# A two-layer hybrid decoder trunk: whole weight blocks in one split, gates ahead of their output block, four query blocks' values in one group

## The chip, the core and the metric

One core of a Trainium2 chip runs the whole program. Five engines work side by side, each through its own instruction stream in order: TensorE (PE: matrix products and transposes), VectorE (DVE), ScalarE (ACT), GpSimd (POOL) and SyncE (SP), which here issues the DMAs. They meet through semaphores that the framework sets from the program's reads and writes. The metric is the device time of one execution in microseconds (us). For the kernel before it is 1511.56 us, the median of three runs from 1508.65 to 1513.46.

## The reference

The input is x (512 positions x 1024 channels, f32) and a memory of 256 tokens. Two layers follow each other, and everything within one reads the same x:

```python
for l in range(2):
    h = x @ w_in[l]            # one wide projection; its columns feed all branches
    (rw_p, rw_g, q_lat, kv_lat, k_pe, mla_g, conv_u, conv_g, xq, xg, merge) = split(h)
    y_rwkv = rwkv7(rw_p, ...) * silu(rw_g)         # 8 heads x 64, recurrent state
    y_mla  = causal_attention(q_lat, kv_lat, k_pe) * silu(mla_g)   # 8 heads
    y_conv = swish(ln(conv31(glu(conv_u)))) * silu(conv_g)         # 31 taps
    y_mem  = cross_attention(xq, mem) * silu(xg)   # 4 heads, 256 memory tokens
    proj   = einsum('bsnc,ncd->bsnd', [y_rwkv, y_mla, y_conv, y_mem], w_o[l])
    gates  = sigmoid(merge.reshape(512, 4, 1024) + b_gate[l])
    merged = sum(gates * proj, axis=2)
    x = layer_norm(alpha * x + merged @ w_out[l])
```

A branch's output is 512 wide. For each of the four branches the merge thus needs eight gate projections (128 channels each, over all 1024 channels of x) and eight output projections (128 channels each, over the branch's 512). The causal attention runs over four blocks of 128 queries; block i reads i + 1 blocks of 128 keys.

## The kernel before, in words

**Precision.** Every large product is f32 made of two parts: a value is split into hi (a cast to the matrix engine's reduced f32) and lo (the rest), and `mm3` issues three matmuls: lo x hi, hi x hi, hi x lo, in some order. So each weight block must be split before it can be used: one cast on ACT for hi, one subtraction on DVE for lo (`split`).

**Layout.** Channels lie on the partitions and the 512 positions on the free axis. A projection of 128 channels (`project`) is eight steps over x's channels, three matmuls of 512 columns each, into one PSUM bank. Weights come from HBM as blocks of 128 x 1024 (128 x 640 for a pair of attention heads, 128 x 672 for the latents, which are called w0 to w3 at the start). `weights` issues the DMA into one of two raw buffers (tag "wr") and splits the block part by part: before, a 1024-column block is two parts of 512, each with its own tile in a ring of six (tags "wh", "wl", `WH = 6`), its own cast and its own subtraction. A raw buffer is free for the next DMA when all parts are split; a slot of the ring is free (`free()`) when the matmuls that use the part have been issued.

**Order.** The order of instructions on each engine is decided when the program is written out. A planner (`Plan`) keeps an estimated clock for each engine, holds a list of tasks (Python generators), and lets the next one emit its instructions by its clocks, due times and the conditions that a task yields. `stream` runs the items (projections, gates, merge blocks) one after another; tasks such as the attention's blocks, the splits, the convolution's taps (`cacc`) or the recurrence are put between their steps. `prefetch`, `get` and `weights` run some blocks ahead of the item that uses them. What an engine got in this order it executes in this order on the chip: an instruction that has to wait holds up all that stand behind it on its engine. A change of a rule or of an instruction's size can therefore move instructions anywhere in the program.

**Attention.** A pair of heads hh (four pairs in each layer) projects pq and pk, casts them to xqh/xql and xkh/xkl, and sends them by DMA into per-head tiles qT and kT. The rotary parts, qrh/qrl, come by DMA too. For each block of 128 queries i and head h, `mla_block` makes scores ms{hh}{h}{i}, a softmax mP{hh}{h}{i}, four or fewer transposes mt{hh}{h}{i} on PE, and a copy of the transposed weights to mPT on ACT. When query blocks 0 and 1 of both heads are done, 6 matmuls of 128 columns go to the output bank mo{hh}, and when blocks 2 and 3 are done, 14 more. The copies go to four buffers of 128 x 512, shared by both heads. The cross-attention's tiles begin with x: xs (scores), xP, xt, xPTh/xPTl, xo; its query projection is ps_xq with outputs xqh/xql too, and its memory projections are ps_mk (keys) and pmv (values).

**Merge.** `merge_items` takes for a branch n (0 recurrence, 1 attention, 2 convolution, 3 memory) and each d2 from 0 to 3 two gate projections ps_m{n}{d} (tanh on ACT into tm{n}{d}, two buffers under the tag "tg") and one block of w_o for two output projections po{n}{d}. DVE then forms (tm + 1) * po and adds it to merged{d}. Before, for d2 = 0 and n other than 3, both gates come first (gate, gate, po, po); in all other places the order is gate, po, gate, po. PSUM has two banks under the name pp for projections (ps_..., po, pmv), two under pa, and four or two under pg for the attention and others.

**End of a layer.** `end_items` opens with `start`, an item of the stream that waits until the recurrence has come far enough ("rwkv"), then issues the DMAs of the residual input and of the norm's parameters at once.

In the profile nearly all ACT, DVE and POOL instructions carry the line of one helper (L235), the matmuls L286, the transposes L291 and the DMAs L298, so work is named by its tiles. Layer 1's names end in _1, layer 0's in _0.

## Time and profile before

| | |
|---|---|
| time, median of three runs | 1511.56 us (1508.65 to 1513.46) |
| the profiled execution's own time | 1509.62 us |
| its span, first to last instruction | 1507.8 us |
| mean granted TensorE clock | 0.998 |
| PE busy | 1475.7 us, 98% of the span |
| PE weight load busy (beside PE) | 1237.5 us, 82% |
| DVE busy | 1072.6 us, 71% |
| ACT busy | 688.1 us, 46% |
| POOL busy | 134.3 us, 9% |
| DMA | 153.54 MB, mean 102 GB/s |

PE is busy nearly the whole time, so only two things move the end: how long PE's own work takes, and the 32 us in which PE stands still. Of these some 6 us lie ahead of its first matmul and some 10 us behind its last. What the other engines do matters only where PE waits for it. The list of what PE waits for names for each wait the tile that PE was about to write and, behind the arrow, the engine and tile that released it. A wait of an engine for PE costs nothing. In a timeline row the columns are the start, the duration, the engine, the operation with its output, inputs and shape, the number of instructions in the row, and in brackets the engine's idle time just before with what ended it. SPq rows are DMA issues.

### The profile page before, as it was taken

To read this page: it belongs to the slowest core of one execution; us is meant where nothing else is said; L and a number is where in the kernel's file an instruction comes from. 1 tells how busy PE (TensorE), PEld (TensorE's weight loads), DVE (VectorE), ACT (ScalarE), POOL (GpSimd) and SP (SyncE) were. 2 spreads that over 40 slices of the span, in tenths; PEclk is the share of its full clock that TensorE was granted. 3 is DMA by queue.
4 is the path that set the end of the run, shared out by engine and by line. 5 is a ranking of instruction groups with operands and counts; after the bars stand their busy time and mean duration, and the time that the engine had idled before them with its cause. 6 is when DMAs were issued, how large, how long until landed. Compare 5 with 4: busy or idle time off the path is not lost.

```text
span 1507.8 us, 29728 instructions
## 1 busy us (share of the span) xinstructions
PE 1475.7 (98%) x11896; PEld 1237.5 (82%) x11896; DVE 1072.6 (71%) x2231; ACT 688.1 (46%) x1507; POOL 134.3 (9%) x329
## 2 busy tenths in 40 slices
PE   8998999999999999999999999999999999999997
PEld 8887788888888888888999877888887888888886
DVE  5787998765758576555554889997866586757847
ACT  5544654345254454444255546533444354444432
POOL 0000000020403021000010000000030202020002
PEclk9999999999999999999999999999999999999999
DMA  6334333223232322433343242432232323234331
GB/s 212 119 115 98 105 100 98 96 77 95 62 86 81 95 88 81 140 98 120 121 144 114 83 126 68 121 109 93 82 98 69 94 74 94 65 104 142 126 119 63
DMA packets 89018, 153.54 MB, mean 102 GB/s; under 512 B 41008, under 2 KB 47152, under 8 KB 88880
## 3 DMA queue, kind: packets, MB, share of 16 engines
q1 hardware_dynamic: 88880, 151.65, 33.9%
q8 instruction: 93, 1.52, 0.4%
q14 instruction: 45, 0.37, 0.1%
HBM read 134.32 MB, written 5.77 MB: 93 GB/s over the span
## 4 chain that ended last, share of the span: by engine, by line
PE 91%; DVE 4%; DMA 2%; ACT 2%; issue 1%; SPq 0%; POOL 0%; ACTq 0%; DVEq 0%; POOLq 0%
PE ps_m L286 23%; PE po L286 12%; PE ps_xg L286 3%; PE ps_cg L286 3%; PE ps_rg L286 3%; PE ps_k L286 3%; PE ps_mg L286 3%; PE ps_v L286 3%; PE ps_r L286 3%; PE ps_val L286 3%; PE ms L286 2%; PE pz L286 2%; PE ps_glu L286 2%; PE ps_xq L286 2%; PE pl L286 2%; PE x L286 2%
## 5 line engine op out<-in xcount | busy, mean ns | idle before, releaser
L235 DVE SCALAR_TENSOR_TENSOR cacc<-hpad,prm,cacc 128x512 f32<-128x512 f32 x240 | 178.8, 747 | 3.3
L235 ACT ACTIVATE tm<-ps_m,prm 128x512 f32<-128x512 f32 x64 | 44.1, 689 | 141.2 <-PE ps_m L286 141.1
L235 DVE SCALAR_TENSOR_TENSOR mt<-tm,po 128x512 f32<-128x512 f32 x48 | 32.9, 686 | 71.2 <-PE po L286 69.0
L235 POOL TENSOR_TENSOR ZT<-ZT,tmpW 64x14 f32<-64x14 f32 (+6 forms) x112 | 42.7, 382 | 8.8
L235 ACT ACTIVATE mP<-ms,nmm 128x512 f32<-128x512 f32 (+3 forms) x64 | 33.7, 528 | 18.2 <-DVE nmm L235 17.4
L235 POOL TENSOR_TENSOR tmpW<-ZT,W 64x14 f32<-64x14 f32 (+6 forms) x112 | 39.3, 351 | 8.1
L235 POOL TENSOR_SCALAR ZT<-W 64x256 f32<-64x256 f32 x8 | 4.2, 524 | 383.8 <-DMA W<-scr 383.8
L235 ACT COPY mPT<-mt 128x512 f32<-128x512 f32 (+3 forms) x64 | 26.7, 428 | 22.2 <-PE mt L291 17.0
L235 DVE TENSOR_TENSOR merged<-merged,mt 128x512 f32<-128x512 f32 x48 | 33.5, 697 | 1.7
L235 POOL MEMSET D<- 128x8 f32 x8 | 1.1, 135 | 346.6 <-PE ms L286 327.1
L235 DVE TENSOR_REDUCE nmm<-ms 128x1 f32<-128x512 f32 (+3 forms) x64 | 29.9, 483 | 0.5
L291 PE MATMUL mt<-cst,mP 128*128 128x128 f32 x160 | 27.1, 277 | 2.4 <-DVE mP L235 2.3
L235 DVE TENSOR_SCALAR mP<-mP,smm 128x512 f32<-128x512 f32 (+3 forms) x64 | 24.8, 387 | 2.3
L235 DVE SCALAR_TENSOR_TENSOR merged<-tm,po 128x512 f32<-128x512 f32 x16 | 11.0, 687 | 20.8 <-PE po L286 19.1
L235 POOL TENSOR_SCALAR lrs<-lmv 128x1 f32<-128x1 f32 x8 | 2.5, 315 | 258.4 <-DVE lmv L235 256.7
L291 PEld LDWEIGHTS mt<-cst,mP 128*128 128x128 f32 x160 | 18.6, 141 | 8.0 <-ACT mo L235 2.2
L235 ACT ACTIVATE z<-z,lnb,lrs 128x256 f32<-128x256 f32 (+1 forms) x16 | 9.6, 648 | 31.1 <-DVE lnb L235 31.1
L235 ACT ACTIVATE yb<-yb,mr,gr 128x64 f32<-128x64 f32 x64 | 22.1, 428 | 2.7 <-DVE mr L235 2.7
L286 PE MATMUL ms<-kTl,qT 96*128 96x512 f32 (+3 forms) x64 | 22.3, 348 | 0.0
L286 PE MATMUL mo<-mPT,v 128*64 128x128 f32 x320 | 21.4, 278 | 0.5 <-ACT mPT L235 0.5
L235 POOL TENSOR_SCALAR gr<-gm 128x8 f32<-128x8 f32 x8 | 1.6, 198 | 215.5 <-DVE gm L235 215.5
L286 PEld LDWEIGHTS mo<-mPT,v 128*64 128x64 f32 x320 | 17.3, 136 | 4.0 <-issue 2.9
(3536 smaller groups left out, 5344.5 us busy)
## 6 DMA issues: line engine op xcount, KB each, us to landing
w<-in_w_ch_dram SPq DMA_DIRECT2D x146, 512.0 KB, 3.7
w<-in_w_o_dram SPq DMA_DIRECT2D x32, 512.0 KB, 3.7
w<-in_w_out_dram SPq DMA_DIRECT2D x16, 512.0 KB, 3.8
w<-in_w_lat_dram SPq DMA_DIRECT2D x16, 336.0 KB, 3.2
w<-in_w_mk_dram SPq DMA_DIRECT2D x8, 512.0 KB, 3.5
w<-in_w_mv_dram SPq DMA_DIRECT2D x8, 512.0 KB, 3.4
w<-in_w_qk_dram SPq DMA_DIRECT2D x8, 320.0 KB, 3.1
x<-in_xT_dram SPq DMA_DIRECT2D x8, 256.0 KB, 5.7
```

Source lines behind the costliest of these rows:

```text
L235: return self.plan.keep(f(*a, **k))
L286: plan.keep(nc.tensor.matmul(o, lhsT, rhs, start=start, stop=stop))
L291: plan.keep(nc.tensor.transpose(o, i, ident))
```

## The change

It has five parts, in one diff.

1. **Splits over the whole block.** A block is one cast and one subtraction over all its columns (up to 1024), into one of three slots of 128 x 1024 (`WH = 3`, the same space). The slot is free when all its parts are used; `free` now takes the tile and counts. The last four blocks of all (w_out, `last`) keep their parts.
2. **Both gates ahead of their output block** in every place of `merge_items`: gate, gate, po, po, and the weight blocks are asked for in that order.
3. **The attention's values of four query blocks in one group**: 20 matmuls to mo{hh} once all eight blocks of a pair are done, not 6 and then 14. The copies go to tiles of 384 columns (blocks 0 and 1, two buffers for each head) and 896 columns (blocks 2 and 3, one buffer for each head); a pair's copies to the latter wait until the pair before it has issued its group.
4. **`turn`** lets a branch's splits start when 8, not 6, outputs of the branch ahead of it are merged.
5. **The end's opening** is a task of its own, and its DMAs are spaced by 3000 and 2000 units of the planner's clock; the stream no longer waits for "rwkv" there.

The order of the emitted instructions shifts in many places. Three of them follow; a name's digits are as in the words above.

ACT, first pair of layer 0, where the copies of the transposed weights mPT of the pair's last blocks (003 and 013) stand beside those of the next pair (1..). Before:

```order
L235 COPY mPT003_0_1684<-mt003_0_1673 128x512
L235 CAST xPTh01_0_1707<-xt01_0_1672 128x512
L235 COPY mPT100_0_1710<-mt100_0_1696 128x128
L235 ACTIVATE mP110_0_1703,smm110_0_1705<-ms110_0_1686,nmm110_0_1704 128x128
L235 COPY mPT013_0_1730<-mt013_0_1712 128x512
L235 ACTIVATE mP101_0_1733,smm101_0_1735<-ms101_0_1723,nmm101_0_1734 128x256
L235 COPY xy0_0_1773<-xo0_0_1732 128x512
L235 ACTIVATE mP111_0_1776,smm111_0_1778<-ms111_0_1737,nmm111_0_1777 128x256
L235 COPY mo0_0_1784<-mo0_0_1365 128x512
```

And now:

```order
L235 COPY mPT002_0_1495<-mt003_0_1542 128x512
L235 CAST xPTh00_0_1572<-xt00_0_1556 128x512
L235 COPY mPT012_0_1529<-mt013_0_1564 128x512
L235 COPY mPT100_0_1577<-mt100_0_1571 128x128
L235 ACTIVATE mP110_0_1615,smm110_0_1617<-ms110_0_1579,nmm110_0_1616 128x128
L235 ACTIVATE mP101_0_1619,smm101_0_1621<-ms101_0_1580,nmm101_0_1620 128x256
L235 COPY mo0_0_1640<-mo0_0_1263 128x512
```

The copy of block 013 now goes into a tile that it shares with block 012 and not into a buffer that an earlier block must give back first; mPT100, which took a buffer ahead of it, comes behind it.

SP, the first two pairs of layer 1, where the DMAs of their queries and keys stand with those of weight block w148. Before:

```order
L298 DMA qTl01_1_10165<-xql_1_10190 64x512
L298 DMA w148_10218<-in_w_ch_dram 128x1024
L298 DMA qT10_1_10224<-qrh0_1_10025 32x512
L298 DMA qTl10_1_10225<-qrl0_1_10026 32x512
L298 DMA qT11_1_10226<-qrh0_1_10025 32x512
L298 DMA qTl11_1_10227<-qrl0_1_10026 32x512
L298 DMA kTh0_1_9283<-xkh_1_10220 64x512
L298 DMA kTh1_1_9285<-xkh_1_10220 64x512
```

And now:

```order
L298 DMA w148_9602<-in_w_ch_dram 128x1024
L298 DMA qT10_1_9611<-qrh0_1_9422 32x512
L298 DMA qTl10_1_9612<-qrl0_1_9423 32x512
L298 DMA qT11_1_9613<-qrh0_1_9422 32x512
L298 DMA qTl11_1_9614<-qrl0_1_9423 32x512
L298 DMA qT00_1_9557<-xqh_1_9585 64x512
L298 DMA qT01_1_9559<-xqh_1_9585 64x512
L298 DMA qTl00_1_9558<-xql_1_9586 64x512
L298 DMA qTl01_1_9560<-xql_1_9586 64x512
L298 DMA kTh0_1_8739<-xkh_1_9607 64x512
```

The weight block and the next pair's rotary queries moved ahead of the first pair's qT, so that nothing but the first pair's own transfers stands between xqh and kT.

ACT, layer 1, the merge of the memory branch (n = 3) at d = 2 and 3, with tanh rows tm32 and tm33 and the convolution's tglu3. Before:

```order
L235 ACTIVATE tm32_1_11770<-ps_m32_1_11727,prm1_8273 128x512
L235 CAST w165h0_11775<-w165_11773 128x512
L235 CAST w165h1_11795<-w165_11773 128x512
L235 CAST w166h0_11802<-w166_11800 128x512
L235 CAST w166h1_11820<-w166_11800 128x512
L235 ACTIVATE tm33_1_11838<-ps_m33_1_11799,prm1_8273 128x512
```

And now:

```order
L235 ACTIVATE tm31_1_10904<-ps_m31_1_10830,prm1_7809 128x512
L235 CAST w161h_10909<-w161_10907 128x1024
L235 CAST w162h_10948<-w162_10946 128x1024
L235 ACTIVATE tglu3_1_10980<-ps_glu3_1_10945 128x512
L235 CAST w163h_11008<-w163_11006 128x1024
L235 CAST lhw_1_10990<-raww_1_10999 128x512
L235 CAST lha_1_10991<-rawa_1_11000 128x512
L235 ACTIVATE tm32_1_11043<-ps_m32_1_11005,prm1_7809 128x512
L235 CAST w164h_11049<-w164_11047 128x1024
L235 ACTIVATE tm33_1_11082<-ps_m33_1_11046,prm1_7809 128x512
```

tglu3, which stood ahead of the whole merge, now stands between tm31 and tm32. It keeps its "tg" buffer until the projection of the convolution's values, which follows this merge on PE, so that tm32 and tm33 take turns in the other one.

The diff's core:

```diff
-WH = 6
+WH = 3
@@ weights
-            for i, (w, c) in enumerate(zip(ws, parts)):
-                if last:
-                    h, lo = (u(f"{name}{n}{i}", 512, F32R) for n in "hl")
-                else:
-                    while wlive["hl"] == WH:
-                        yield lambda: wlive["hl"] < WH
-                    wlive["hl"] += 1
-                    h = wp.tile([128, 512], F32R, tag="wh", name=f"{name}h{i}")[:, 0:c]
-                    lo = wp.tile([128, 512], F32R, tag="wl", name=f"{name}l{i}")[:, 0:c]
-                yield from split(h, lo, raw[:, e:e + c])
...
+            else:
+                while len(wlive["hl"]) == WH:
+                    yield lambda: len(wlive["hl"]) < WH
+                h, lo = (wp.tile([128, 1024], F32R, tag=f"w{n}", name=f"{name}{n}") for n in "hl")
+                wlive["hl"][h.tensor.name] = len(parts)
+                yield from split(h[:, 0:cols], lo[:, 0:cols], raw)
+                for w, c in zip(ws, parts):
+                    w.extend((h[:, e:e + c], lo[:, e:e + c]))
+                    e += c
@@ free
-    def free(n=1):
-        wlive["hl"] -= n
+    def free(h):
+        n = h.tensor.name
+        wlive["hl"][n] -= 1
+        if wlive["hl"][n] == 0:
+            del wlive["hl"][n]
@@ mla_block
-            if i > 1:
-                PT = m("mPT" + q, 512, "mPT", 4)
-            else:
-                if h not in two:
-                    two[h] = m("mPT" + q, 512, "mPT", 4)
-                PT = two[h][:, 128 * i:]
-            PT = two[h, i] = PT[:, 0:n]
-            S.copy(PT, ps)
+            if (h, i // 2) not in two:
+                if L["pairs"] < hh - 1 + i // 2:
+                    yield lambda: L["pairs"] >= hh - 1 + i // 2
+                two[h, i // 2] = m("mPT" + q, 896, f"mPW{h}", 1) if i > 1 else m("mPT" + q, 384, f"mPT{h}", 2)
+            e = (0, 128, 0, 384)[i]
+            S.copy(two[h, i // 2][:, e:e + n], ps)
...
-            if len(done) < 4:
+            if len(done) < 8:
                 return
             yield "small"
-            for b in (i - i % 2, i - i % 2 + 1):
+            for b in range(4):
@@ turn
-            return n == 3 or added[{1: 3, 2: 1, 0: 2}[n]] >= 6
+            return n == 3 or added[{1: 3, 2: 1, 0: 2}[n]] >= 8
@@ merge_items
-                        while len(ts) <= (1 if d2 == 0 and n != 3 else b):
+                        while len(ts) < 2:
                             ts.append((yield from gate(get, 2 * d2 + len(ts))))
...
-                blocks = [(A["w_ch"][l, CH_M + 8 * n + 2 * d2], (512, 512)), (A["w_o"][l, n, d2], (512, 512)), (A["w_ch"][l, CH_M + 8 * n + 2 * d2 + 1], (512, 512))]
-                if d2 == 0 and n != 3:
-                    blocks = [blocks[0], blocks[2], blocks[1]]
+                blocks = [(A["w_ch"][l, CH_M + 8 * n + 2 * d2], (512, 512)), (A["w_ch"][l, CH_M + 8 * n + 2 * d2 + 1], (512, 512)), (A["w_o"][l, n, d2], (512, 512))]
@@ end_items
             def start(get):
+                plan.spawn(opening())
+                yield
+
+            def opening():
                 yield lambda: "rwkv" in L
...
                     for i in range(zn):
                         DMA(E["z"][tb][i], TOK[l][:, tb, zw * i:zw * i + zw])
+                    plan.t += 3000.0
+                    yield
```

More of the change, by code (lines that the diff above doesn't have):

```diff
@@ L428, in split @@
         V.tensor_tensor(out=dst_l, in0=src, in1=dst_h.bitcast(F32), op=ALU.subtract)
-    wlive = {"raw": 0, "hl": 0}
+    wlive = {"raw": 0, "hl": {}}
     def weights(name, src, parts, last=False):
@@ L442, in run @@
             e = 0
-            for i, (w, c) in enumerate(zip(ws, parts)):
-                if last:
-                    h, lo = (u(f"{name}{n}{i}", 512, F32R) for n in "hl")
-                else:
-                    while wlive["hl"] == WH:
-                        yield lambda: wlive["hl"] < WH
-                    wlive["hl"] += 1
-                    h = wp.tile([128, 512], F32R, tag="wh", name=f"{name}h{i}")[:, 0:c]
-                    lo = wp.tile([128, 512], F32R, tag="wl", name=f"{name}l{i}")[:, 0:c]
-                yield from split(h, lo, raw[:, e:e + c])
-                e += c
-                w.extend((h, lo))
+            if last:
+                for i, (w, c) in enumerate(zip(ws, parts)):
+                    h, lo = (u(f"{name}{n}{i}", c, F32R) for n in "hl")
+                    yield from split(h, lo, raw[:, e:e + c])
+                    e += c
+                    w.extend((h, lo))
+                    yield
[7 more added lines that the diff above has]
+                    w.extend((h[:, e:e + c], lo[:, e:e + c]))
+                    e += c
                 yield
@@ L486, in project @@
             if k % 4 == 3:
-                free()
+                free(h)
             if k < 7:
@@ L502, in wide @@
                     yield
-            free()
+            free(h)
     def narrow(get, cols, blocks, name, lhs, after):
@@ L517, in narrow @@
                 if b == blocks - 1 and k % 2:
-                    free()
+                    free(h)
                 if k in (1, 3, 5):
@@ L1278, in run @@
                             yield
-                    free()
+                    free(h)
                 if nb == 0:
@@ L1374, in token_blocks @@
                     if tb == 3:
-                        free()
+                        free(w[i][0])
                 yield
@@ L1440, in run @@
                         yield
-                    free()
+                    free(w[0])
                     plan.spawn(heads(T, ps, n, s, there))
@@ L1464, in pair @@
             yield
-            left = [2]
+            two, done = {}, []
             for i in range(4):
-                if i % 2 == 0:
-                    two, done = {}, []
                 for h in range(2):
@@ L1472, in pair, with mla_block @@
                     L["jobs"] += 1
-                    plan.spawn(mla_block(hh, h, i, (qT[h], kT[h]), mo, two, done, left))
+                    plan.spawn(mla_block(hh, h, i, (qT[h], kT[h]), mo, two, done))
                     yield
             L["turn"] += 1
-        def mla_block(hh, h, i, T, mo, two, done, left):
+        def mla_block(hh, h, i, T, mo, two, done):
             n = 128 * i + 128
@@ L1512, in mla_block @@
             done.append(q)
-            if len(done) < 4:
+            if len(done) < 8:
                 return
             yield "small"
-            for b in (i - i % 2, i - i % 2 + 1):
+            for b in range(4):
                 for kb in range(b + 1):
                     for half in range(2):
+                        e = (0, 128, 0, 384)[b] + 128 * kb
                         MM(mo[HALF[half], 128 * b:128 * b + 128], vtok[kb][:, 128 * hh + 64 * half:128 * hh + 64 * half + 64],
-                           two[half, b][:, 128 * kb:128 * kb + 128], start=kb == 0, stop=kb == b)
-            left[0] -= 1
-            if left[0] == 0:
-                L["pairs"] += 1
-                yield
-                yo = u(f"mo{hh}" + t_)
-                S.copy(yo, mo)
-                pg.free()
-                ymla.append(yo)
-                if len(ymla) == 4:
-                    close_phase()
-                    L["mla"] = True
+                           two[half, b // 2][:, e:e + 128], start=kb == 0, stop=kb == b)
+            L["pairs"] += 1
+            yield
+            yo = u(f"mo{hh}" + t_)
+            S.copy(yo, mo)
+            pg.free()
+            ymla.append(yo)
+            if len(ymla) == 4:
+                close_phase()
+                L["mla"] = True
         merged = [None] * 8
@@ L1598, in run @@
                                 yield
-                        free()
+                        free(wh)
                         if merged[d] is None:
@@ L1641, in start @@
             def start(get):
+                plan.spawn(opening())
+                yield
+            def opening():
                 yield lambda: "rwkv" in L
@@ L1649, in start @@
                         DMA(E["z"][tb][i], TOK[l][:, tb, zw * i:zw * i + zw])
+                    plan.t += 3000.0
+                    yield
                 def affine(ll):
@@ L1657, in affine @@
                             res.append(b)
+                            plan.t += 2000.0
+                            yield
                     return res
@@ L1661, in start @@
                 if l:
-                    ab = affine(l - 1)
+                    ab = yield from affine(l - 1)
                     def residual():
@@ L1684, in start @@
                 if last:
-                    E["ab"] = affine(l)
+                    E["ab"] = yield from affine(l)
             def ahead(get):
```

## The prediction

> **What bounds the kernel now.** I read the page's first part, then the list of what PE waits for, then the timelines around the longest of those waits.

> ```profile
> span 1507.8 us, 29728 instructions
> PE 1475.7 (98%) x11896; PEld 1237.5 (82%) x11896; DVE 1072.6 (71%) x2231; ACT 688.1 (46%) x1507; POOL 134.3 (9%) x329
> ```

> PE has work for 98% of the span; the rest, 32.1 us, is all that better order can win. The waits say where it lies:

> ```profile
> PE pl L286 <- DVE w0l L235: 6.2, 1, 6.2
> PE pq L286 <- DVE xql L235: 2.4, 1, 2.4
> PE mt L291 <- DVE mP L235: 2.3, 2, 1.8
> PE xo L286 <- DVE xPTl L235: 2.1, 2, 1.6
> PE pmv L286 <- DVE w126l L235: 1.7, 1, 1.7
> PE xs L286 <- ACT xqh L235: 0.9, 1, 0.9
> PE mo L286 <- ACT mPT L235: 0.5, 1, 0.5
> ```

> The columns after the colon are the total in us, how many times, and the longest. No row names a gate ps_m or an output po: PE never waits in the merge. There the others wait for PE:

> ```profile
> L235 ACT ACTIVATE tm<-ps_m,prm 128x512 f32<-128x512 f32 x64 | 44.1, 689 | 141.2 <-PE ps_m L286 141.1
> L235 DVE SCALAR_TENSOR_TENSOR mt<-tm,po 128x512 f32<-128x512 f32 x48 | 32.9, 686 | 71.2 <-PE po L286 69.0
> ```

> So the change can act on the end in three ways only: PE's own time where its operations change places, the waits above, and new waits.

> **The change, part by part.**

> *Whole-block splits.* They take about 240 instructions each off ACT and DVE (the order has 1253 rows on ACT before and 1016 after, 1924 and 1675 on DVE). Nearly all of that lies beside PE. What it does to a block that PE waits for is seen at the start:

> ```profile
> 5.09 0.47 ACT L235 CAST w0h<-w 128x336 fp32r<-128x336 f32 x1 [0.61 <-DMA w<-in_w_lat_dram]
> 5.59 0.51 DVE L235 TENSOR_TENSOR w0l<-w,w0h 128x336 fp32r<-128x336 f32 x1 [0.39 <-ACT w0h L235]
> 6.16 0.65 PE L286 MATMUL pl<-w0l,xh 128*128 128x336 f32 x1 [6.16 <-DVE w0l L235]
> ```

> Cast, subtraction, first matmul stand in a row. With 672 columns both get longer. The slopes come from here and from the next fence (512 columns: cast 0.62, subtraction 0.68): (0.62 - 0.47) / 176 = 0.85 ns a column for ACT, (0.68 - 0.51) / 176 = 0.97 for DVE. Another 336 columns cost 0.29 + 0.32 = **+0.6 us**, in front of everything. A block of 1024 then takes about 0.62 + 0.43 = 1.05 us on ACT and 0.68 + 0.49 = 1.17 on DVE.

> *Pair 0 of layer 0, 2.4 us of waiting.* PE cannot start the next pair's pq until xqh and xql have emptied the bank:

> ```profile
> 101.57 0.33 SPq L298 DMA_DIRECT2D w<-in_w_ch_dram  x1
> 107.51 0.62 ACT L235 CAST w25h<-w 128x512 fp32r<-128x512 f32 x1 [1.65 <-DMA w<-in_w_ch_dram]
> 108.34 0.59 ACT L235 ACTIVATE xqh<-pq 128x512 fp32r<-128x512 f32 x1
> 108.96 0.69 DVE L235 SCALAR_TENSOR_TENSOR xql<-pq,xqh 128x512 fp32r<-128x512 f32 x1 [1.84 <-ACT xqh L235]
> 109.57 0.68 DVE L235 TENSOR_TENSOR w25l<-w,w25h 128x512 fp32r<-128x512 f32 x1
> ```

> The cast of w25, waiting for its DMA, stands ahead of xqh in ACT's queue. After the change it still does, now whole, and w25l, whole, stands ahead of xql on DVE, where it stood behind. If the DMA lands as late, xql moves from 108.96 to about 107.51 + 1.05 + 1.17 = 109.73: +0.8. But w22 to w24 are now split in one go each, which gives the raw buffer back earlier, by one cast, one subtraction and the task between them; an estimate is 1 to 2 us. Ends: +0.8 and -2.4. I take **-0.6**, nearest to the DMA coming 1.4 earlier.

> *Memory values of layer 1, 1.7 us.* PE waits for the first half of w126l:

> ```profile
> 773.82 1.13 ACT L235 CAST w126h<-w 128x512 fp32r<-128x512 f32 x2
> 774.55 1.29 DVE L235 TENSOR_TENSOR w126l<-w,w126h 128x512 fp32r<-128x512 f32 x2
> ```

> Now it waits for the whole: the cast ends at 773.82 + 1.05 = 774.87, 0.3 later than DVE turns to w126l now, and the subtraction takes 1.17 in place of the first half's 0.68. **+0.8** (ends 0 and +1.2).

> [...]

> *One group of values.* A group of 128 x 64 matmuls costs PE more than its matmuls:

> ```profile
> 907.18 0.88 PE L286 MATMUL mo<-mPT,v 128*64 128x128 f32 x12
> 907.99 0.55 PE L291 MATMUL mt<-cst,mP 128*128 128x128 f32 x3
> ...
> 933.30 0.39 PE L286 MATMUL ps_xg<-xh,w150h 128*128 128x512 f32 x1
> 933.52 0.40 PE L286 MATMUL ps_xg<-xh,w150l 128*128 128x512 f32 x1
> 933.85 1.75 PE L286 MATMUL mo<-mPT,v 128*64 128x128 f32 x28
> 935.53 0.50 PE L286 MATMUL pq<-ltl,w151h 128*128 128x512 f32 x1
> ```

> Each matmul shows as two records. 28 records take 935.53 - 933.85 = 1.68 us until the next starts, 12 take 0.81: 54 ns a record, and 0.16 over. On entry the step is 0.33 where a 512-column matmul otherwise takes 0.22 to 0.23: 0.10 more. So about 0.25 for each group, and 16 groups become 8: **-2.0** (ends -1.6 and -3.0).

> *The copies of the weights.* The knot of the first pair:

> ```profile
> 145.01 0.59 ACT L235 COPY mPT<-mt 128x512 f32<-128x512 f32 x1 [3.91 <-PE mo L286]
> 146.10 0.16 DVE L235 RECIPROCAL smm<-smm 128x1 f32<-128x1 f32 x1 [2.96 <-ACT mP L235]
> 145.65 1.09 PE L286 MATMUL mo<-mPT,v 128*64 128x128 f32 x14 [0.46 <-ACT mPT L235]
> 149.82 0.41 PE L291 MATMUL mt<-cst,mP 128*128 128x128 f32 x2 [1.80 <-DVE mP L235]
> ```

> A copy waits 3.91 us until an earlier group has given back one of the four buffers; behind it stand the next softmax rows, DVE idles for them, and PE loses 0.46 and then 1.80. In the new order block 013 has its place in a tile that is open, so this wait has nothing to wait for: **-2.3** (ends 0 and -2.3). New is the wait on the pair before for the 896-column tiles; a copy that is kept back there holds its PSUM bank, but it is kept back in the writing, so nothing stands behind it on ACT. The xs wait (0.9) belongs to scores that now come one step later on PE: **-0.9** (ends 0 and -0.9).

> *Start of the attention in layer 1.* Here SP is what is late:

> ```profile
> 880.36 1.16 SPq L298 DMA_DIRECT2D qT<-xqh  x2
> 888.57 1.19 SPq L298 DMA_DIRECT2D qT<-xqh  x2
> 888.62 0.60 ACT L235 ACTIVATE xkh<-pk 128x512 fp32r<-128x512 f32 x1 [3.68 <-DMA qT<-qrh]
> 892.45 0.59 ACT L235 CAST xPTh<-xt 128x512 fp32r<-128x512 f32 x1 [1.33 <-DMA qT<-xqh]
> 894.49 0.50 PE L286 MATMUL xo<-xPTl,vmh 128*128 128x512 f32 x1 [1.56 <-DVE xPTl L235]
> ```

> SP issues about one DMA each 0.6 us from 880 to 895, ACT waits for those transfers, and PE loses 2.1 us at xo. With w148 and the second pair's four rotary transfers ahead, the chain is five issues shorter, some 3 us. I take **-1.6** of the 2.1 (ends 0 and -2.1). Against it, w148's cast of 1.05 us now stands between xqh and xkh: **+0.4** of it (ends 0 and +1.05).

> *Gates first.* No wait goes away, for there was none. One new wait is in the order: in layer 1 tm32 and tm33 take turns in one buffer since tglu3 sits in the other, and po32 and po33 fall into one PSUM bank. po33 must wait until DVE has read po32: 0.69 for that operation (the row mt above) and about 0.3 for the hand-over on both sides. **+1.0** (ends 0 and +1.7, when tm33's 0.69 comes on top).

> *turn and the opening.* Splits of y and the residual's DMAs move by microseconds in the order's middle, where the other engines wait for PE. **+0.3** for a convolution gate that comes sooner behind the attention (ends 0 and +1.0).

> Sum: 0.6 - 0.6 + 0.8 - 2.0 - 2.3 - 0.9 - 1.6 + 0.4 + 1.0 + 0.3 = **-4.3 us**. The profiled execution took 1509.62, so it would take 1505.3; the median of the three runs stands 1.94 above it, and I forecast from the median: 1511.56 - 4.3 = 1507.3, **1507.2**. A measurement of this kernel can tell about 0.3%, 4.5 us, from no change, so the forecast stands just at that edge.

> **The rivals.**

> *Stalls only move, no net change.* The planner's clock put PE's waits where it did not see them; a new order has new ones. For it: the seven waits above follow no rule but collisions of one DMA or one buffer. Then of the sum only what is certain stays, start and groups, 0.6 - 2.0 = -1.4, with some new waits of 1 to 2 us: about 1511.

> *Slower: a whole block at the head of ACT's queue.* One mechanism, at each of the eight starts of a pair: the cast now takes the whole block, and DVE the whole subtraction, ahead of xqh/xql. The price of one is in the pair-0 rows: 2.4 as it was and 0.7 more, 3.1. For it: w25 and w148 in the order. Against it: before, the same wait came up once in eight pairs, and raw buffers now come free earlier. From three such starts on it decides (-4.3 + 9.3 = +5.0); with five, 1507.2 + 15.5 = 1522.7.

> *Faster by more: the lighter helpers carry through.* About 240 blocks save 0.12 us each on DVE (1.29 against 1.17), 29 us in all, and ACT saves some; then DVE, busy for 71%, comes before PE at nearly each place where it is late now. PE's waits on DVE other than the first, 2.4 + 2.3 + 2.1 + 1.7 = 8.5 in the rows above, would go whole, where the sum takes 0.6 + 2.3 + 1.6 - 0.8 = 3.7 of them: 4.8 more, 1502.4. Against it: those waits hang on a DMA, a buffer and SP, not on DVE's load. The rows bear this out little. [...]

> **How the numbers follow.** The sum's case, within 4 us of 1507.2, 0.50: just over half of it, 0.29, is beyond 0.3% and 0.21 within. More than that faster (the third rival among it), 0.13. No net change, 0.17. Slower, 0.20. Together faster 0.42, same 0.38, slower 0.20. The range leaves out the slow rival's larger part and the last of the fast: 1500 is the third rival with the groups at their -3.0 and the pair-0 wait gone whole; 1515 holds two pair starts with a new wait of 3.1 and one of half that (1507.2 + 7.7). The likeliest case's own range is 1503 to 1511.

> **What would show it.** In the profile after: the first matmul at about 6.8; eight groups mo of 40 records each; no row of mo on mPT or of mt on mP above 1 us; the wait at xo below 0.6; pmv on w126l at 2.5; a new row of po on DVE's merged of about 1 us; pq on xql below 2; DVE and ACT each some 15 to 25 us less busy, PE's busy time about 2 us less. It would be wrong if PE's waits for xqh, xql, xPTl or a weight's lo add up to more than the 11 us of before: then whole blocks hold up the queues.

## The result, and the profile after

The changed kernel takes 1506.12 us (median of 7 runs, 1504.40 to 1506.81), the one before 1511.56 (7 runs, 1508.65 to 1513.46). The ratio is 0.9971, 95% interval 0.9961 to 0.9980: faster by 0.29%, some 4.4 us (the two medians differ by 5.4). Forecast were 1507.2 and -4.3. The size came out; how the sum got there is another matter, and the runs below were made for it.

The page of the kernel after (span, busy time and share of each engine), against 1507.8 and 1475.7, 1072.6, 688.1 before:

```profile
span 1504.9 us, 29132 instructions
PE 1474.2 (98%) x11896; PEld 1239.7 (82%) x11896; DVE 1053.5 (70%) x1994; ACT 662.1 (44%) x1270; POOL 137.1 (9%) x329
```

DVE is 19 us less busy, ACT 26, PE 1.5. What PE waits for in the kernel after:

```profile
PE pl L286 <- DVE w0l L235: 6.7, 1, 6.7
PE pmv L286 <- DVE w126l L235: 2.6, 1, 2.6
PE tk L291 <- DVE S L235: 1.8, 1, 1.8
PE pq L286 <- DVE xql L235: 1.6, 2, 0.9
PE ps_xq L286 <- DVE xql L235: 1.4, 2, 0.9
PE ps_glu L286 <- DVE xql L235: 1.1, 1, 1.1
...
PE po L286 <- DVE merged L235: 0.8, 1, 0.8
PE ps_mg L286 <- DVE xql L235: 0.6, 1, 0.6
```

The rows mt, mo, xo and xs are gone. pmv has grown, and po and ps_glu, ps_mg and pq at other starts of pairs are new. All of PE's waits behind its first matmul add up to 13.7 us, against 15.7 before: much of what was won was lost again elsewhere. The second longest wait behind the first matmul's, tk (a transpose of the recurrence, 1.8), is new too: it is there in all seven kernels of this document that have part 2, at 1.6 to 1.8, and in none of the seven others. The forecast has no term for it.

A group of values in the kernel after, 8 of which there are:

```profile
922.30 0.40 PE L286 MATMUL ps_xg<-xh,w150l 128*128 128x512 f32 x1
922.63 2.40 PE L286 MATMUL mo<-mPT,v 128*64 128x128 f32 x40
924.96 0.50 PE L286 MATMUL ps_xg<-xl,w150h 128*128 128x512 f32 x1
```

40 records take 924.96 - 922.63 = 2.33 us; 12 and 28 took 0.81 + 1.68 = 2.49, and one of two entries (0.10) is gone too. That is 0.26 for a pair, 2.1 for eight.

### The profile page after: what moved, and what is told of

Read it like the earlier page. It is cut to its first block, busy times and chain, and to the rows that moved or that the text cites. A ratio compares the mean times of both kernels' runs of the same rounds, so it can differ in the third digit from the quotient of the medians.

```text
span 1504.9 us, 29132 instructions
## 1 busy us (share of the span) xinstructions
PE 1474.2 (98%) x11896; PEld 1239.7 (82%) x11896; DVE 1053.5 (70%) x1994; ACT 662.1 (44%) x1270; POOL 137.1 (9%) x329
## 4 chain that ended last, share of the span: by engine, by line
PE 90%; DVE 5%; ACT 2%; issue 1%; DMA 1%; POOL 0%; SPq 0%; ACTq 0%; POOLq 0%; DVEq 0%
PE ps_m L286 23%; PE po L286 11%; PE ps_xq L286 3%; PE ps_v L286 3%; PE ps_xg L286 3%; PE ps_cg L286 3%; PE ps_rg L286 3%; PE ps_k L286 3%; PE ps_mg L286 3%; PE ps_r L286 3%; PE ps_val L286 3%; PE ps_glu L286 2%; PE ms L286 2%; PE pl L286 2%; PE pz L286 2%; PE pmv L286 2%
## 5 line engine op out<-in xcount | busy, mean ns | idle before, releaser
L235 DVE SCALAR_TENSOR_TENSOR cacc<-hpad,prm,cacc 128x512 f32<-128x512 f32 x240 | 179.2, 749 | 3.9
L235 ACT ACTIVATE tm<-ps_m,prm 128x512 f32<-128x512 f32 x64 | 44.1, 689 | 166.6 <-PE ps_m L286 156.1
L235 DVE SCALAR_TENSOR_TENSOR mt<-tm,po 128x512 f32<-128x512 f32 x48 | 32.9, 686 | 89.9 <-PE po L286 89.6
L235 POOL TENSOR_TENSOR tmpW<-ZT,W 64x14 f32<-64x14 f32 (+6 forms) x112 | 42.7, 381 | 7.8
L235 POOL TENSOR_TENSOR ZT<-ZT,tmpW 64x14 f32<-64x14 f32 (+6 forms) x112 | 42.0, 375 | 8.8
L235 ACT ACTIVATE mP<-ms,nmm 128x128 f32<-128x128 f32 (+3 forms) x64 | 33.6, 529 | 20.3 <-DVE nmm L235 19.5
L235 POOL TENSOR_SCALAR ZT<-W 64x256 f32<-64x256 f32 x8 | 3.6, 447 | 369.7 <-DMA W<-scr 369.7
L235 ACT COPY mPT<-mt 128x128 f32<-128x128 f32 (+3 forms) x64 | 26.1, 428 | 19.6 <-PE mt L291 19.4
L235 DVE TENSOR_TENSOR merged<-merged,mt 128x512 f32<-128x512 f32 x48 | 33.6, 699 | 1.7
L235 POOL MEMSET D<- 128x8 f32 x8 | 0.9, 116 | 342.7 <-PE ms L286 321.2
L235 DVE TENSOR_REDUCE nmm<-ms 128x1 f32<-128x128 f32 (+3 forms) x64 | 30.0, 484 | 0.1
L235 POOL TENSOR_SCALAR lrs<-lmv 128x1 f32<-128x1 f32 x8 | 3.6, 447 | 253.6 <-DVE lmv L235 252.2
L235 DVE TENSOR_SCALAR mP<-mP,smm 128x128 f32<-128x128 f32 (+3 forms) x64 | 24.8, 387 | 2.3
L291 PE MATMUL mt<-cst,mP 128*128 128x128 f32 x160 | 25.9, 273 | 0.0
L235 DVE SCALAR_TENSOR_TENSOR merged<-tm,po 128x512 f32<-128x512 f32 x16 | 11.0, 687 | 20.1 <-PE po L286 20.0
L235 ACT ACTIVATE z<-z,lnb,lrs 128x256 f32<-128x256 f32 (+1 forms) x16 | 9.6, 647 | 30.1 <-DVE lnb L235 30.1
L235 POOL TENSOR_SCALAR gr<-gm 128x8 f32<-128x8 f32 x8 | 2.4, 298 | 224.0 <-DVE gm L235 224.0
L235 ACT ACTIVATE yb<-yb,mr,gr 128x64 f32<-128x64 f32 x64 | 22.1, 434 | 1.1 <-DVE mr L235 1.1
L286 PE MATMUL ms<-kTl,qT 96*128 96x128 f32 (+3 forms) x64 | 22.3, 348 | 0.0
L291 PEld LDWEIGHTS mt<-cst,mP 128*128 128x128 f32 x160 | 19.0, 141 | 3.6 <-ACT xP L235 0.2
L235 ACT ACTIVATE xP<-xs,nmx 128x256 f32<-128x256 f32 x32 | 15.1, 473 | 13.7 <-DVE nmx L235 11.2
L286 PE MATMUL ms<-kTh,qT 96*128 96x128 f32 (+3 forms) x64 | 20.6, 322 | 0.0
```

What stands on the lines that cost most here:

```text
L235: return self.plan.keep(f(*a, **k))
L286: plan.keep(nc.tensor.matmul(o, lhsT, rhs, start=start, stop=stop))
L291: plan.keep(nc.tensor.transpose(o, i, ident))
```

## The experiments

A program built from the changed one with parts undone has an order of its own, and not each combination was run. Those below include one path from before to after, one part at a time: part 4 (turn), then 3 (group), 1 (split), 2 (gates), 5 (opening). The runs were timed in three batches, each on another chip and in five rounds beside the kernel before: e1 to e4 (its median there 1509.43), e5 to e8 (1510.32) and e9 to e12 (1509.14). Each ratio is to the kernel before in the same batch, so that ratios, not medians, compare across batches. The row "changed" is the result above.

| run | parts in it | median us | ratio to before | 95% interval |
|---|---|---|---|---|
| e1_turn | 4 | 1508.66 | 0.9997 | 0.9986 to 1.0009 |
| e2_group | 4, 3 | 1504.96 | 0.9971 | 0.9963 to 0.9980 |
| e3_split | 4, 3, 1 | 1507.21 | 0.9990 | 0.9981 to 0.9999 |
| e4_gates | 4, 3, 1, 2 | 1505.32 | 0.9974 | 0.9964 to 0.9984 |
| changed | all | 1506.12 | 0.9971 | 0.9961 to 0.9980 |
| e5_parts | 4, 3, half of 1 | 1508.23 | 0.9986 | 0.9974 to 0.9997 |
| e6_two | all, three blocks in two parts | 1508.03 | 0.9986 | 0.9977 to 0.9995 |
| e7_nogroup | all but 3 | 1507.26 | 0.9983 | 0.9974 to 0.9992 |
| e8_nogates | all but 2 | 1507.92 | 0.9986 | 0.9978 to 0.9995 |
| e9_w0 | all, w0 in two parts | 1504.97 | 0.9971 | 0.9958 to 0.9983 |
| e10_pmv | all, w0 and w126 in two parts | 1502.22 | 0.9955 | 0.9942 to 0.9969 |
| e11_late | 4, 3, 5 | 1504.42 | 0.9970 | 0.9959 to 0.9981 |
| e12_both | as e10_pmv without 5 | 1503.89 | 0.9960 | 0.9948 to 0.9972 |

0.001 of the ratio is 1.5 us. A difference quoted below is one of ratios where nothing else is said. With intervals of about 0.001 on each side, a difference of 2 us between two rows is near the limit of what can be told.

**e1_turn.** Part 4 alone:

```diff
-            return n == 3 or added[{1: 3, 2: 1, 0: 2}[n]] >= 6
+            return n == 3 or added[{1: 3, 2: 1, 0: 2}[n]] >= 8
```

> The kernel before with part 4 alone (8 merged outputs, not 6, before a branch's splits may start). The sum theory gives this part about nothing: within 1 us of before. The theory that new orders bring new waits of their own (stalls only move) expects single us either way, 0 to +3, even for this small edit.

Measured -0.0003: nothing that can be told.

**e2_group.** Part 3 on top of it:

```diff
-            if len(done) < 4:
+            if len(done) < 8:
```

and the copies' tiles with it, as in the diff of the change.

> The run before this one and part 3, the attention's values in one group. Sum theory: -2.0 for eight groups less, -2.3 for the copy that waited 3.91 us, -0.9 for xs, so about -5 against the turn-only kernel, and the mt and mo rows gone from PE's waits. Theory that the lighter helpers carry the gain: only the -2.0 of the groups. Theory that stalls only move: -2.0 and new waits, 0 to -2.

Measured 0.9997 to 0.9971: -3.9 us, between the sum's -5 and the groups' -2.0. What PE waits for in this kernel, with one wait of mt left of 0.4 and none of mo:

```profile
PE pq L286 <- DVE xql L235: 2.2, 1, 2.2
PE pmv L286 <- DVE w126l L235: 1.7, 1, 1.7
PE xo L286 <- DVE xPTl L235: 1.6, 1, 1.6
...
PE mt L291 <- DVE mP L235: 0.4, 1, 0.4
```

The knot went, as worked out. The xs wait (0.7) stayed at this step; e11_late, which lacks parts 1 and 2, has it too (1.1), and e3_split does not. So it went with part 1 and not, as forecast, with the groups.

**e3_split.** Part 1 on top of that.

```diff
-                yield from split(h, lo, raw[:, e:e + c])
+                yield from split(h[:, 0:cols], lo[:, 0:cols], raw)
```

with three slots of 1024 columns.

> The run before this one and part 1, whole-block splits. Sum theory: +0.6 at the start, +0.8 at pmv, -0.6 at pq, -1.6 and +0.4 at the start of the attention in layer 1, so -0.4 in all. Theory that whole blocks at the head of ACT's queue hold up the starts of pairs: +3 or more, with PE waiting for xql at three pair starts or more. Lighter helpers: -4 or more.

Measured 0.9971 to 0.9990: +2.9 us; the two intervals just do not touch. By the medians of the batch it is +2.2, and by the median span +2.0: some executions of e3_split took up to 5.0 us beyond their span, those of the kernel before 1.8. So slower is clear, and the size good to about 1 us. My sum had -0.4. PE's waits in this kernel:

```profile
PE pl L286 <- DVE w0l L235: 6.6, 1, 6.6
PE pmv L286 <- DVE w126l L235: 2.6, 1, 2.6
PE ps_m L286 <- DVE w213l L235: 2.3, 1, 2.3
PE pq L286 <- DVE xql L235: 2.2, 2, 1.4
PE x L286 <- DVE T L235: 1.5, 1, 1.5
PE ps_glu L286 <- DVE xql L235: 1.1, 1, 1.1
...
PE ps_mg L286 <- DVE xql L235: 0.6, 1, 0.6
```

The start and pmv have their +0.6 and +0.9. New are a gate that waits for its weight's lo (2.3), and waits for xql at starts of pairs. The gate's wait, on DVE in this kernel:

```profile
1340.33 0.69 DVE L235 SCALAR_TENSOR_TENSOR mt<-tm,po 128x512 f32<-128x512 f32 x1 [5.60 <-PE po L286]
1341.05 0.69 DVE L235 TENSOR_TENSOR merged<-merged,mt 128x512 f32<-128x512 f32 x1
1341.66 1.22 DVE L235 TENSOR_TENSOR w213l<-w,w213h 128x1024 fp32r<-128x1024 f32 x1
```

DVE stood idle for 5.6 us with mt at its head, which waits for po on PE. Behind mt stands the subtraction of w213, which PE needs for the gate that follows that po at once. Its cast had ended at 1339.17, so without mt ahead of it the subtraction could have started 2.5 us earlier. The cast was late for a like reason: on ACT it stood behind tm, which waited 6.55 us for ps_m on PE. So these waits for PE were not free: PE lost the 2.3 us by them. The order gate, po, gate, po makes this possible wherever the second gate's weight is split late; in this kernel it happened at one place.

**e4_gates.** Part 2 on top of that.

```diff
-                        while len(ts) <= (1 if d2 == 0 and n != 3 else b):
+                        while len(ts) < 2:
```

> The run before this one and part 2, both gates ahead of their output block; only the opening's part is then missing to the changed kernel. Sum theory: +1.0 from the new wait of po on DVE's merged, no other wait in the merge. Against it: if the gates-first order gives ACT and DVE time for the splits, less than 0.

Measured 0.9990 to 0.9974: -2.4 us (the intervals overlap by a little; -1.9 by the medians). The wait of 2.3 is gone, po on merged is there at 0.8, and tk on S at 1.8; x on T (1.5) is gone. The sum's sign was wrong.

**e8_nogates**, the same step undone in the kernel with all other parts.

```diff
-                        while len(ts) < 2:
+                        while len(ts) <= (1 if d2 == 0 and n != 3 else b):
```

> The changed kernel without part 2: gate, po, gate, po. My sum had the gates-first order cost 1.0, so this should be 1 faster. From e3_split and e4_gates I now expect the other sign: with whole blocks in three slots the output block holds one slot across the second gate, whose block then comes late; 1 to 3 us slower, with a wait of ps_m on a weight's lo.

Measured 0.9986 against 0.9971 of the changed kernel: 2.3 us slower (the intervals overlap a little), with ps_m on w213l at 2.3 again. So the row came and went with part 2 twice, and the time each time by about as much.

**e7_nogroup**, part 3 undone in the kernel with all other parts:

```diff
-            if len(done) < 8:
+            if len(done) < 4:
```

> The changed kernel without part 3: two groups of values for a pair again, four copy buffers. If the group's gain (3.7 us between e1_turn and e2_group) is the groups' and the copies' own, it is lost here too: 3 to 5 us over the changed kernel, of which 2 from eight groups more, and PE waits for mo or mt again. If the gain hung on the old splits, within 1 us.

Measured 0.9983 against 0.9971: 1.8 us slower, with overlapping intervals, and less than the 3 us expected. The only row of the knot's kind is mt on mo at 0.4. Its 16 groups take 0.81 and 1.68 us again, so the groups' price by the rows is the same here; the time agrees with it but does not prove it. The copies' knot belongs to the order of the kernel before: with the new order of the splits it did not come up, even with four copy buffers.

**e5_parts.** e3_split with its slots of 1024 columns, but each part cast and subtracted by itself:

```diff
-                yield from split(h[:, 0:cols], lo[:, 0:cols], raw)
+                for w, c in zip(ws, parts):
+                    yield from split(h[:, e:e + c], lo[:, e:e + c], raw[:, e:e + c])
```

> The kernel e3_split (parts 1, 3 and 4) with its three slots of 1024 columns kept, but each block cast and subtracted in its two parts, one instruction each, as before. If the loss of part 1 comes from whole blocks at the head of the queues, this gives it back: 1504 to 1505.5, PE's waits for xql, w126l and w0l as in e2_group. If it comes from the coarser slots (a slot is free only when both halves are used), it stays at 1507 and the wait of ps_m on w213l with it.

Measured 0.9986: 0.6 us less than e3_split, 2.3 more than e2_group (another batch). PE's waits in it:

```profile
PE mt L291 <- DVE smx L235: 2.6, 2, 1.7
PE xo L286 <- DVE xPTl L235: 2.1, 2, 1.6
PE pmv L286 <- DVE w126l L235: 1.4, 2, 0.8
PE g_1x L286 <- DVE kt L235: 1.2, 1, 1.2
...
PE pq L286 <- DVE xql L235: 0.6, 1, 0.6
```

The waits for the weights' halves went back as the first theory says, w213l is gone, and the total is the same: other waits stand in their place. At mt, PE waits for softmax rows that stand on DVE behind the halves w28l and w29l. Neither theory has it. What this run shows is that a new order has waits of this total size of its own; "stalls only move" holds between e3_split and e5_parts.

**e6_two.** The changed kernel with w0, w125 and w126 in two parts:

```diff
+                if name in ("w0", "w125", "w126"):
+                    for w, c in zip(ws, parts):
+                        yield from split(h[:, e:e + c], lo[:, e:e + c], raw[:, e:e + c])
```

> The changed kernel with three blocks alone (w0, w125 and w126) cast and subtracted in two parts; PE's order is otherwise nearly the same. My start term says the first matmul comes 0.6 earlier, my pmv term that the wait falls by 0.8 to 0.9, so -1.5 against the changed kernel, and -2.7 if the slow matmuls behind the pmv wait go too: about 1504. If both are hidden elsewhere: no difference.

Measured 0.9986, 2.3 us more than the changed kernel: a miss. The first matmul came 0.7 earlier. But the planner put the second half of w126 behind the next weight block, on ACT as on DVE. DVE in this kernel:

```profile
766.18 0.68 DVE L235 TENSOR_TENSOR w126l<-w,w126h 128x512 fp32r<-128x512 f32 x1
768.89 0.69 DVE L235 TENSOR_TENSOR xl<-xf,xh 128x512 fp32r<-128x512 f32 x1 [2.03 <-ACT xh L235]
769.50 0.85 DVE L235 TENSOR_TENSOR w127l<-w,w127h 128x672 fp32r<-128x672 f32 x1
770.27 0.69 DVE L235 TENSOR_TENSOR w126l<-w,w126h 128x512 fp32r<-128x512 f32 x1
```

So PE waits twice, 2.4 and 1.6 us. And PE's matmuls behind the first wait are slow:

```profile
766.92 0.58 PE L286 MATMUL pmv<-w126l,memh 128*128 128x256 f32 x1 [2.41 <-DVE w126l L235]
767.30 0.42 PE L286 MATMUL pmv<-w126h,memh 128*128 128x256 f32 x1
767.52 0.41 PE L286 MATMUL pmv<-w126h,meml 128*128 128x256 f32 x1
...
777.14 0.29 PE L286 MATMUL pmv<-w126l,memh 128*128 128x256 f32 x1
```

Starts 0.21 us apart in place of 0.12, until 777.1: 24 such steps, 2.3 us more for them alone. This led to the next pair.

**e9_w0** and **e10_pmv.** The order of PE is the changed kernel's, and so is that of ACT and DVE but for w2's subtraction and the parts themselves; w0 in two parts, and in e10_pmv alone, by the second branch, also w126 in two parts that stay next to each other:

```diff
+                if name == "w0":
+                    for w, c in zip(ws, parts):
+                        yield from split(h[:, e:e + c], lo[:, e:e + c], raw[:, e:e + c])
...
+                elif name in ("w126",):
+                    m = parts[0]
+                    S.copy(h[:, 0:m], raw[:, 0:m])
+                    S.copy(h[:, m:cols], raw[:, m:cols])
+                    yield
+                    for x in (slice(0, m), slice(m, cols)):
+                        V.tensor_tensor(out=lo[:, x], in0=raw[:, x], in1=h[:, x].bitcast(F32), op=ALU.subtract)
```

> The changed kernel with the first block w0 alone cast and subtracted in two parts; every other instruction in the same order. My start term: first matmul 0.6 us earlier and the end with it, -0.6. A rival from the earlier runs: the first 3 us of matmuls run slow in any case, so an earlier start only moves slow matmuls: -0.3 or less.

> As e9_w0, and w126 cast twice and subtracted twice in a row at the same place in ACT's and DVE's order; PE's order is that of the changed kernel. The first half of w126l is there about 0.5 us earlier, so the pmv wait falls from 2.6 to about 2.1. If only the wait counts: 0.5 less than e9_w0. If a long wait there is what sets the clock back for some 13 matmuls in most executions: the slow matmuls go in part of them too, and the granted clock rises by about 0.001 (1.3 us): 1 to 1.8 less than e9_w0.

e9_w0: the first matmul stands at 6.0 in place of 6.7, but the ratio is the changed kernel's, 0.9971; 0.7 us lie inside both intervals. e10_pmv: 0.9955, 2.4 us less than e9_w0 by the medians' ratios, with overlapping intervals. The wait is 1.7 again:

```profile
768.15 0.38 PE L286 MATMUL pmv<-w126l,memh 128*128 128x256 f32 x1 [1.70 <-DVE w126l L235]
768.37 0.28 PE L286 MATMUL pmv<-w126h,memh 128*128 128x256 f32 x1
```

0.9 less, and the matmuls behind it start 0.12 us apart. The rest goes with the clock: e10_pmv's five runs had granted clocks of 0.998 four times and 0.996 once (that one took 1505.37), e9_w0's eight between 0.995 and 0.998, 0.9961 in the mean. That fits the second theory; with five runs and overlapping intervals it does not prove it. e10_pmv has the lowest ratio of all here, clearly below before; its interval overlaps the changed kernel's.

**e11_late.** e2_group with the opening as a task (the main lines):

```diff
             def start(get):
+                plan.spawn(opening())
+                yield
```

> The kernel e2_group (parts 3 and 4) with part 5, the opening as a task: the changed kernel without whole-block splits and without gates first. My sum gave part 5 0 to +0.3; e4_gates against the changed kernel gave no difference. If parts 1 and 2 together cost nothing, this equals the changed kernel; 1504 to 1506.

Measured 0.9970, the changed kernel's and e2_group's: part 5 is worth nothing that can be told (to some 1.5 us either way), and parts 1 and 2 together nothing.

**e12_both.** e10_pmv's edits on e4_gates (the main lines, against e10_pmv):

```diff
             def start(get):
-                plan.spawn(opening())
-                yield
```

> The kernel e4_gates (all but part 5) with the two small edits of e10_pmv. If part 5 is worth nothing it equals e10_pmv; as the sum of what the runs have shown it should be the fastest, about 1 to 2 under the changed kernel.

Measured 0.9960: e10_pmv's within the intervals, and not faster, as had been expected of it.

## Why the prediction was right, and where it was not

**The total was right because two terms erred in opposite ways.** Along the path, in us: turn -0.5 (forecast about 0), group and copies -3.9 (forecast -5.2: -2.0, -2.3, -0.9), splits +2.9 (forecast -0.4), gates -2.4 (forecast +1.0), opening -0.5, none of it told from zero (turn and opening together +0.3 forecast). Splits and gates add up to +0.5 against a forecast of +0.6. All of the gain is there with parts 4 and 3 alone (e2_group, 0.9971); parts 1, 2 and 5 add nothing that can be told.

In part that is luck. Beside the terms of the sum the profile after has 5.5 us of waits that no term names (tk 1.8, ps_glu 1.1, pq at 878 us 0.75, ps_xq 0.7 more at 883, ps_mg 0.6, pz 0.6), where the forecast put +0.4; and several waits fell by more than their terms (pq, mt, mo, xo), or fell without one (ps_xq at 162 us by 1.0, ps_val by 0.7).

The forecast's own sign of being wrong did not come: PE's waits for xql and for a weight's lo, behind the first matmul, are 8.5 us. For the kernel before the rows give 10.2 with xqh and xPTl, not quite the 11 named.

**Groups: right, in mechanism and size.** 2.1 us by the rows, forecast 2.0; undoing it last cost 1.8, which agrees within wide intervals.

**The copies' knot: right.** mt at 1.8 and mo at 0.5 went with part 3. e7_nogroup adds that it was no lasting cost of four buffers but a collision in one order, and e5_parts, which has part 3, that PE can wait there again (mt 2.6) behind other instructions. **xs: wrong in its cause.** The row went, but with part 1.

**Start: right as a row.** The first matmul at 6.75, forecast 6.8. Taking it back changed the time by less than could be told.

**pmv: the wait was right, its price was not.** It grew from 1.70 to 2.57, +0.9 for a forecast of +0.8. In the profile of the kernel after, the matmuls behind it then run slow:

```profile
769.68 0.40 PE L286 MATMUL pmv<-w126l,memh 128*128 128x256 f32 x1 [2.57 <-DVE w126l L235]
769.91 0.39 PE L286 MATMUL pmv<-w126h,memh 128*128 128x256 f32 x1
```

The first 40 matmuls and transposes from here on take 6.38 us in this profile and 4.86 in that of e4_gates, where the same wait of 2.57 was not followed by slow ones: 1.5 us, which no term held.

**Pair 0's pq: too small.** The DMA did land earlier, by 2.66 us: the cast of w25 starts at 104.85, not 107.51, at a place that PE reaches 0.4 earlier. The wait of pq there went from 2.4 to 0.9, -1.5 for a forecast of -0.6. ACT in the kernel after:

```profile
104.85 1.05 ACT L235 CAST w25h<-w 128x1024 fp32r<-128x1024 f32 x1 [0.70 <-DMA w<-in_w_ch_dram]
105.80 0.59 ACT L235 ACTIVATE xqh<-pq 128x512 fp32r<-128x512 f32 x1
```

The cast's price of 1.05 was as worked out; the subtraction of w25 behind it on DVE takes 1.22, where 1.17 was worked out.

**Start of the attention in layer 1: won and lost, and the loss at another engine.** xo's 2.1 went whole (forecast -1.6); it is gone in e3_split and back in e5_parts, so it went with the whole blocks. But PE waits for xql 0.75 at pq and 0.86 at ps_xq. The forecast gave 0.4 to w148's cast between xqh and xkh on ACT. That cast is there, but no wait hangs on xkh; what holds up xql is DVE. In the kernel after, DVE, with xqh done at 876.33:

```profile
876.04 1.22 DVE L235 TENSOR_TENSOR w147l<-w,w147h 128x1024 fp32r<-128x1024 f32 x1
877.18 0.69 DVE L235 TENSOR_TENSOR xy<-xy,xg 128x512 f32<-128x512 f32 x1
877.78 0.69 DVE L235 SCALAR_TENSOR_TENSOR xql<-pq,xqh 128x512 fp32r<-128x512 f32 x1
879.81 1.22 DVE L235 TENSOR_TENSOR w148l<-w,w148h 128x1024 fp32r<-128x1024 f32 x1
```

The subtraction of a whole block stands ahead of xql; w148l stands in the same way ahead of the instruction on DVE that releases the second pair's xqh. With halves in e5_parts there is no such wait at pq, and 0.16 at ps_xq.

**The step that failed** is "Gates first. No wait goes away, for there was none." That was read from the profile of before, in which the order gate, po, gate, po met splits in halves. With whole blocks the same order makes ps_m wait 2.3 us on w213l (e3_split, e8_nogates); gates first takes that away. The new wait of po on merged was there, 0.8 for the forecast 1.0: PE's last matmul for the po before ends at 1013.50, DVE runs from 1013.53 to 1014.22, and PE goes on at 1014.27. DVE's 0.69 is as forecast; the hand-over is 0.03 and 0.05 by these rows, where the forecast had an estimate of 0.3. I priced each part against the kernel before and added up; two of them had a price only together. In the sum of all five parts this cancels; it shows on the path alone.

**The slow rival was a smaller truth.** Whole blocks at the heads of queues do hold up starts of pairs: PE's waits for xql in the kernel after are 4.7 us at pq, ps_xq, ps_glu and ps_mg, against 2.4 + 1.5 and two of xs before. But no single one of them reaches the 3.1 that the rival's price took, and ps_glu's 1.1 is there with halves too (e5_parts), so not all of it is the whole blocks'. *Stalls only move* is what e3_split and e5_parts look like side by side. *Lighter helpers* fell: from e2_group to e3_split DVE and ACT have 46 us less work, and the kernel got slower.

What stays open: why e5_parts has other waits of the same total. A kernel with halves and six slots together with gates first was not run, so what gates first does without whole blocks is not shown. And why tk comes with part 2 was not followed up.

## What to carry over

On a kernel whose bound engine is busy for 98% of the span, price the parts of a change in the order in which they are put on, not each against the kernel before: a part that "removes no wait" may remove one that another part brings. Look for a wait of another engine at the head of an in-order queue (here mt, 5.6 us idle on DVE), and ask what stands behind it. And a pause of the matrix engine can cost more than its length: here 2.57 us of waiting, and 1.5 more when the clock was set back behind it.

## What the hardware showed that I had not expected

The traces show what went with it. In each of the 14 profiles all changes of the granted clock lie on one grid of steps of 3.41 us: in the kernel after at 12.16, 769.92, 773.33 and 1496.96 us, which are 222, 1 and 212 steps of 3.413 apart, in the kernel before at 12.31 and 1500.53, 436 steps apart. The place of that grid differs from execution to execution: the borders of the rows below, taken back by whole steps, give a first one at 1.92 us in the kernel after, 2.08 in the one before, 2.80 in e4_gates and 3.31 in e8_nogates. The rows are steps of the grid: first time, length, then PE's busy time; the granted clock is the third number from the end. The kernel after, whose wait lies whole within one step:

```profile
766.51:769.92 3.41, 0.84 (x8) 0.60 (x7) 2.11 (x3) 3.35 (x6) 0.00 (x0) 1.00 0.74 288
769.92:773.33 3.41, 3.41 (x18) 3.41 (x18) 1.33 (x2) 0.82 (x3) 0.00 (x0) 0.50 0.61 158
```

e4_gates, where a border of the grid cuts the same wait in two:

```profile
763.97:767.38 3.41, 2.07 (x17) 1.60 (x15) 1.40 (x3) 3.22 (x6) 0.00 (x0) 1.00 1.01 390
767.38:770.79 3.41, 2.04 (x17) 2.04 (x18) 2.74 (x3) 2.31 (x5) 0.00 (x0) 1.00 0.45 149
770.79:774.21 3.42, 3.42 (x31) 3.42 (x31) 1.79 (x3) 2.60 (x5) 0.00 (x0) 1.00 0.40 120
```

The closest cases on both sides, e8_nogates with a wait of 1.90 and the kernel before with its wait of 2.42 at pq, of which 1.82 lie in this step:

```profile
1348.16:1351.57 3.41, 1.51 (x33) 1.32 (x32) 0.85 (x3) 0.28 (x2) 0.00 (x0) 1.00 0.05 16
1351.57:1354.98 3.41, 3.41 (x59) 2.57 (x61) 0.93 (x3) 0.37 (x2) 0.00 (x0) 0.50 0.02 5
```

```profile
107.89:111.30 3.41, 1.59 (x7) 1.33 (x8) 2.34 (x5) 2.03 (x5) 0.00 (x0) 1.00 0.33 74
```

From the clock's first rise (at 9 to 12 us; in the kernel after at 12.16, where the starts of the 336-column matmuls go from 0.28 to 0.16 us apart) to PE's last matmul, seven steps at full clock in the 14 profiles have PE idle for 1.90 us or more, and a step at half clock follows each of them; no step at full clock with 1.82 or less is followed by one. In one place shorter waits added up: of the waits of 0.94 and 1.67 at 145 to 148 us in e5_parts 2.2 us lie in one step, and a slow one follows. So in these profiles a single wait below 1.9 did not set the clock back, and for a longer one it went with where the grid fell. In e6_two the slow stretch lasts three steps (10.24 us); why is open.

The scatter between runs of one kernel goes with the clock. Of 33 runs of the kernel before, those with a mean granted clock of 0.998 took 1508.2 (median of 3), those with 0.996 1510.8 (10), those with 0.994 1514.4 (3). In e10_pmv no pause behind the first matmul is over 1.8 us, and four of its five runs have 0.998. One kernel does not fit: e7_nogroup has the wait of 2.6, and eight of its eleven runs have 0.998 too. That single waits make the scatter is thus likely, but not shown.
